# Fixed engine orders at two layer borders, and expert weights loaded in pieces of 4 MB

## The chip, the core and the metric

The kernel runs on one core of a Trainium2 chip. The core has five engines that each work off a queue of instructions of their own: TensorE (PE, matmuls; its weight loads are listed as PEld), VectorE (DVE), ScalarE (ACT), GpSimd (POOL) and SyncE (SP), which here issues nearly all DMAs. The metric is the time of one execution on the device in microseconds; less is better. All data is float32, x is 256 tokens of 1024 features, and all weights are read from HBM once, 503 MB in all.

## The reference, cut to what matters

Two transformer blocks one after another. The first mixes by a gated unit and a forgetting attention and ends in a gated feed-forward layer; the second mixes by pooling, an mLSTM and attention, then attends to a memory of 256 tokens, and ends in 16 experts, each of which takes the 32 tokens that score highest for it.

```python
# block 1
h = rmsnorm(x, mix_pre_g);  proj = h @ w_in
...
x = x + rmsnorm(merged @ w_out, mix_post_g)
h = rmsnorm(x, ffn_pre_g)
x = x + rmsnorm((silu(h @ w_gate) * (h @ w_up)) @ w_down, ffn_post_g)
# block 2
hn = rmsnorm_2(x, norm_mix_g);  proj = hn @ w_in_2
...
x = x + concatenate([y_pool, y_mlstm, y_attn]) @ w_out_2
x = x + mem_cross_attn(rmsnorm_2(x, norm_mem_g), mem, ca_wq, ca_wkv, ca_wo)
x = x + ec_moe(rmsnorm_2(x, norm_ffn_g), router_w, w_gu, w_down)
return rmsnorm_2(x, final_norm_g)

def expert(xe, wgu, wd):              # xe 32 x 1024, wgu 1024 x 4096, wd 2048 x 1024
    ga, up = split(xe @ wgu, 2)
    return (silu(ga) * up) @ wd
```

Between a norm and its product stands a whole row of x: a token's 1024 features must be summed in square before any of them can be scaled.

## The kernel before

**Dense layers.** x stays in SBUF as two tiles of 128 tokens (t = 0, 1). Weights come in units of 1 MB through three raw slots (`unit`, `unit_c`, lines 47 to 57), all on SP's queue. Each unit is split into a high and a low part by `split` (line 59): ACT copies the high part (line 67, in two halves), DVE subtracts it for the low part (line 68). The split units (`whl`) lie in four slots called hl. A product is made in three passes, high by high, low by high, high by low (`mm3`, line 86), with activations split in the same way (xh, xl). A norm (`norm_T`) squares on ACT (line 151), makes one over the root on DVE (`rstd`, lines 127 to 133: a guess on the bits and three steps of refinement, nine small operations and, with the sum at line 153, ten), scales x to hn (line 172), and has PE transpose hn (line 185); lines 118 and 119 copy the transposes into xh and xl.

**The two borders.** At border 1 (`block1_mix`, from line 414) the merged mixer output is multiplied by w_out for t = 0, then t = 1; each result goes through a norm (square, `pn` at line 201, rstd), is added to x (line 209), and is normalised again for the feed-forward layer. Beside it PE multiplies two units of block 2's memory keys (`mem_K`, tiles memH and memL), work that depends on nothing here. At border 2 (end of `block1_ffn`, line 577, and `block2_mix`, line 650) the same happens between the last three units of the down product (`tail`) and the first projections of block 2: keys and values (wk), then queries (wq), each for both tiles. After each of them ACT copies the result (lines 654 to 658).

**What sets the order.** A scheduler orders the instructions of each engine, from the order of the code and its own estimate of when each is ready; `queued` and the list `behind` (line 71) hold single instructions behind a named one. Engines wait for each other by semaphores.

**The experts.** `moe` (line 1068) has twelve slots of 2 MB (16 KB in each of 128 partitions): eight pools of its own and the four hl. `eload` (line 1088, issue at line 1091) puts the loads on SP's queue in one fixed order: for each expert eight of gate and up (128 rows of 16 KB each), then four of down. A slot is loaded again when PE is done with it. Per gate-and-up load PE does 16 matmuls (line 1163), on tokens that were gathered by matmuls with a one-hot matrix (line 1145). Then come silu and product (lines 1183, 1184), transposes (line 1187), the down products (line 1196) and the scatter back to the tokens (line 1210). The last expert's downs are loaded in pieces (line 1243): for three of the four the first 512 columns, then the rest, in rows of 2 KB; the fourth in four column cuts, so that little is left to do behind the last load. Then the final norm and two stores (line 1262).

## Time and profile before

| | |
|---|---|
| median of 3 runs | 1532.17 us (1532.10 to 1532.32) |
| the profiled execution | 1532.34 us, of which 1530.6 us lie between first and last instruction (the span) |
| mean granted TensorE clock | 0.890 |
| PE busy | 1194.9 us, 78% of the span |
| DVE, ACT busy | 430.8 us (28%), 349.6 us (23%) |
| moved by DMA | 503.0 MB, mean 329 GB/s |
| chain that ended last | 54% DMA, 2% PE, 2% SP's queue, 1% DVE |

The busy shares are means over stages that differ. Up to about 575 us PE is busy nearly throughout and the DMA moves 110 to 300 GB/s; from about 610 us the DMA moves 426 to 430 GB/s in each slice of the page and PE is busy for about 60% of the time. The chain is followed back from the last instruction, so its DMA share is the stage of the experts. Times in the trace count from the span's start. "Idle before" at a row is the time for which the engine had nothing to do ahead of it, and behind the arrow stands what ended that.

### The profile page before, as it was taken

The numbers are of one execution on the slowest core, as the hardware profiler recorded it, in microseconds if no ns is written. First come the engines' busy times: TensorE is split into PE (matmuls) and PEld (weight loads), VectorE is DVE, ScalarE is ACT, GpSimd is POOL, SyncE is SP. The second block draws the span as 40 slices with busy tenths as digits, with TensorE's granted clock in tenths as the row PEclk, the third lists the DMA queues.
The fourth block names the chain that finished last, engine by engine and source line by source line (L and its number), as shares of the span: only waits on it lengthen the run. The fifth ranks groups of instructions, "written<-read, shape, count | busy, mean of one in ns | idle before, by whom it ended". The sixth has DMA issues, their size and how long they took to land.

```text
span 1530.6 us, 17896 instructions
## 1 busy us (share of the span) xinstructions
PE 1194.9 (78%) x7704; PEld 677.5 (44%) x7704; DVE 430.8 (28%) x840; ACT 349.6 (23%) x604; POOL 7.0 (0%) x19
## 2 busy tenths in 40 slices
PE   7999998999999999886766666756656666567665
PEld 5988988999978786321121111111111112111112
DVE  6744666544577764300000000000000000000002
ACT  6554544443456733000000000000000000000002
POOL 1000000000000000000000000000000000000000
PEclk9999999999999999998877868789887789787798
DMA  9754446655533369999999999999999999999996
GB/s 302 223 165 147 156 150 220 193 187 187 178 114 109 111 235 429 399 428 426 427 428 427 428 427 428 426 429 426 428 426 428 426 428 428 426 428 426 428 424 245
DMA packets 109103, 503.00 MB, mean 329 GB/s; under 512 B 10059, under 2 KB 64095, under 8 KB 84960
## 3 DMA queue, kind: packets, MB, share of 16 engines
q1 hardware_dynamic: 109024, 501.86, 82.4%
q8 instruction: 60, 0.98, 0.3%
q14 instruction: 19, 0.16, 0.0%
HBM read 500.79 MB, written 1.05 MB: 328 GB/s over the span
## 4 chain that ended last, share of the span: by engine, by line
DMA 54%; PE 2%; SPq 2%; DVE 1%; issue 0%; ACT 0%; DVEq 0%
DMA eraw<-in_expert_w_gu_dram 36%; DMA eraw<-in_expert_w_down_dram 18%; SPq L1243 2%; PE sm L1163 1%; PE sm L1196 1%; PE sm L1145 0%; DVE tk L1117 0%; DVE m L1116 0%; PE acc L1210 0%; DVE OH L1129 0%; DVE x L1252 0%; ACT L1183 0%; PE sm L1187 0%; DVE es L1184 0%; DVE eraw L1260 0%
## 5 line engine op out<-in xcount | busy, mean ns | idle before, releaser
L1163 PE MATMUL sm<-eraw,xs 128*32 128x512 f32 x2048 | 323.9, 741 | 192.7 <-DMA eraw<-in_expert_w_gu_dram 192.7
L1163 PEld LDWEIGHTS sm<-eraw,xs 128*32 128x32 f32 x2048 | 62.4, 122 | 427.0 <-DMA eraw<-in_expert_w_gu_dram 291.9
L1196 PE MATMUL sm<-eraw,aT 128*32 128x512 f32 (+2 forms) x1088 | 173.4, 774 | 79.9 <-DMA eraw<-in_expert_w_down_dram 71.7
L68 DVE TENSOR_TENSOR whl<-raw,whl 128x1024 fp32r<-128x1024 f32 x166 | 198.8, 1220 | 113.2 <-ACT whl L67 112.5
L67 ACT ACTIVATE whl<-raw 128x1024 fp32r<-128x1024 f32 x166 | 168.3, 1052 | 84.7 <-issue 59.0
L1184 DVE SCALAR_TENSOR_TENSOR es<-sm,rsl,es 128x512 f32<-128x512 f32 x16 | 12.0, 751 | 465.6 <-PE sm L1163 462.6
L1196 PEld LDWEIGHTS sm<-eraw,aT 128*32 128x32 f32 x1088 | 34.7, 130 | 200.4 <-DMA eraw<-in_expert_w_down_dram 119.7
L1183 ACT ACTIVATE es<-sm,rsl 128x512 f32<-128x512 f32 x16 | 11.0, 687 | 426.8 <-PE sm L1163 426.8
L86 PE MATMUL acc<-xh,whl 128*128 128x256 f32 x704 | 95.6, 283 | 0.0
L86 PE MATMUL sm<-xh,whl 128*128 128x256 f32 x704 | 92.6, 284 | 1.1 <-ACT xh L118 1.1
L86 PEld LDWEIGHTS sm<-xh,whl 128*128 128x128 f32 x704 | 89.0, 192 | 1.9 <-ACT xh L118 1.3
L86 PEld LDWEIGHTS acc<-xh,whl 128*128 128x128 f32 x704 | 87.8, 189 | 1.1
L1208 DVE COPY ys<-sm 128x512 f32<-128x512 f32 (+2 forms) x18 | 11.4, 631 | 237.4 <-PE acc L1210 233.0
L86 PE MATMUL acc<-whl,xh 128*128 128x512 f32 x256 | 70.1, 404 | 1.1 <-DVE whl L68 0.8
L1210 PE MATMUL acc<-ys,ogT 128*128 128x512 f32 (+2 forms) x136 | 66.4, 612 | 5.1 <-DVE ys L1208 4.3
L1206 ACT ACTIVATE ys<-sm 128x512 f32<-128x512 f32 x16 | 9.6, 597 | 229.6 <-PE sm L1196 229.6
L86 PE MATMUL acc<-whl,aH 128*128 128x512 f32 x176 | 55.8, 390 | 0.0
L86 PEld LDWEIGHTS acc<-whl,xh 128*128 128x128 f32 x256 | 47.1, 189 | 14.2 <-DVE whl L68 2.2
L86 PE MATMUL acc<-xl,whl 128*128 128x256 f32 x352 | 49.7, 281 | 0.0
L86 PE MATMUL sm<-xl,whl 128*128 128x256 f32 x352 | 49.7, 284 | 0.0
L1210 PEld LDWEIGHTS acc<-ys,ogT 128*128 128x128 f32 x136 | 23.8, 198 | 53.2 <-issue 21.1
L86 PEld LDWEIGHTS sm<-xl,whl 128*128 128x128 f32 x352 | 45.6, 192 | 0.0
(364 smaller groups left out, 1098.4 us busy)
## 6 DMA issues: line engine op xcount, KB each, us to landing
eraw<-in_expert_w_gu_dram SPq DMA_DIRECT2D x128, 2048.0 KB, 39.2
eraw<-in_expert_w_down_dram SPq DMA_DIRECT2D x60, 2048.0 KB, 39.3
raw<-in_w_in_dram SPq DMA_DIRECT2D x34, 1024.0 KB, 5.4
raw<-in_w_gate_dram SPq DMA_DIRECT2D x11, 1024.0 KB, 5.4
raw<-in_w_up_dram SPq DMA_DIRECT2D x11, 1024.0 KB, 5.4
raw<-in_w_down_dram SPq DMA_DIRECT2D x11, 1024.0 KB, 5.0
raw<-in_w_out_dram SPq DMA_DIRECT2D x8, 1024.0 KB, 5.2
eraw<-in_expert_w_down_dram SPq DMA_DIRECT2D x7, 1024.0 KB, 27.7
```

What stands on the lines that cost most here:

```text
L67: nc.scalar.activation(H[:, k], raw[:, k], AF.Copy)
L68: self.at["L"] = nc.vector.tensor_tensor(L[:, k], raw[:, k], H[:, k].bitcast(F32), OP.subtract).ins
L86: nc.tensor.matmul(out, l[i], r[j], start=first and p == 0 and q == 0, stop=last and p == 2 and q == n - 1)
L1163: nc.tensor.matmul(dst[32 * j:32 * j + 32, :], xs[:, k, 32 * q:32 * q + 32], raw[:, o + 512 * j:o + 512 * j + 512], start=k == 0, stop=k = ...
L1183: nc.scalar.activation(s, G, AF.Silu, scale=rs)
L1184: nc.vector.scalar_tensor_tensor(s, U, rs, s, OP.mult, OP.mult)
L1196: nc.tensor.matmul(y[c0][32 * c:32 * c + 32, 0:n], aT[:, c, 32 * j:32 * j + 32], raw[:, o:o + n], start=j == 0, stop=j == 3, tile_position ...
L1206: nc.scalar.activation(ys, y[c0][:, 0:n], AF.Copy)
L1208: nc.vector.tensor_copy(ys, y[c0][:, 0:n])
L1210: nc.tensor.matmul(out[t], ogT[:, t * 128:(t + 1) * 128], ys, start=first, stop=last)
L1243: nc.sync.dma_start(raws[j].rearrange("p (i n) -> p i n", i=4)[:, :, c0:c0 + m], rows(j)[:, :, c0:c0 + m])
```

## The change

**Borders.** `strict()` ties each PE, DVE and ACT instruction that is written inside it to the one before it on its engine, so that the code's order is the engine's order. The code at both borders is written out anew in that order. Splits are placed half by half (`half_H`, `half_L`), a key unit's halves around the transposes of tile 1, and `rstd_q` takes the place of the bit guess: ACT makes the root, DVE a reciprocal and one step of refinement, five DVE operations and one ACT operation. At border 1 the raw weights of both key units and of the first gate unit are loaded ahead, and the first key unit is split before tile 1's out-projection. At border 2 the second key-and-value unit gets a split slot of its own (`whx`, pool `hx`), and the query product of tile 0 is cut in two around the transposes of tile 1.

**Experts.** The features are numbered anew (`feats`): piece k of x is every second column of a block of 256, so that two neighbouring pieces are the even and the odd rows of 256 rows of the weights. The pieces of experts 0 and 1 are still 2 MB in rows of 16 KB, now 32 KB apart in HBM. From expert 2 on one load brings two pieces, 4 MB in 128 rows of 32 KB; the eight pools are closed and four of 32 KB are opened in their place, and the four hl take the four downs. The router's weights and the gain are loaded in the same numbering. Of the last expert, downs 0 and 1 are loaded whole, in rows of 16 KB, and are used in all columns at once.

```diff
+def feats(k):
+    o = 256 * (k // 2) + k % 2
+    return slice(o, o + 255, 2)
...
+    def strict(self):
+        traced = self.nc.cur_bb.bb.instructions
...
+        for i in traced[start:]:
+            if i.engine in engines:
+                if at[i.engine] is not None:
+                    self.tc.add_manual_dep(i, at[i.engine].name, mybir.DependencyInfo(
+                        mybir.DependencyClass.NoSync, mybir.DependencyReason.DATA), reason="strict")
+                at[i.engine] = i
...
+    def rstd_q(self, ss):
...
+        nc.vector.tensor_scalar(v, ss[:, 0:1], ss[:, 1:2], 1.0 / D, OP.add, OP.mult)
+        nc.scalar.activation(d, v, AF.Sqrt, bias=self.eps)
+        nc.vector.tensor_scalar(h, v, -0.5, -0.5 * EPS, OP.mult, OP.add)
+        nc.vector.reciprocal(y, d)
+        nc.vector.tensor_scalar(t, y, y, h, OP.mult, OP.mult)
+        nc.vector.tensor_scalar(y, t, 1.5, y, OP.add, OP.mult)
...
+            raws = [self.unit_c(a["ca_wkv_2"][0], 256 * i) for i in range(2)] + [self.unit_c(a["w_gate"][0], 0)]
+            with self.strict():
...
+                self.post_norm_c(1, y, self.rstd_q(ss))
+                w.append(self.split_tile(raws[1]))
+                for i in range(2):
+                    self.split_half(w[1], raws[1], i)
+                ss = self.squares(self.xh(1))
+                self.mem_K(0, (w[0][:, 0], w[0][:, 1]))
+                ps = self.trans_ps(hs[0], "acc")
+                self.trans_H(xT[0], ps, 0)
+                hs[1] = scale(1, self.work.tile([128, D], F32, name="hn", tag="work"), self.rstd_q(ss))
+                kT = self.ps("sm")
+                self.mem_K_half(kT, 0, (w[1][:, 0], w[1][:, 1]))
...
+            HL = [self.split_tile(raws[0]), self.sb(self.hx, [128, 2, 4, 512], "whx", F32R)]
...
+            with self.strict():
+                out_k(0, self.gemm_t(xT, wk, 0))
+                acc = self.ps("acc")
+                self.gemm_part(acc, xT, wq, 0, 0)
+                ps = self.trans_ps(h, "sm")
+                self.trans_H(xT[0], ps, 1)
+                for q in range(2):
+                    self.trans_L(*xT, ps, 1, q)
+                self.gemm_part(acc, xT, wq, 0, 1)
...
+                if e == 2:
+                    est.close()
+                    e_ = [(self.open("ee%d" % i, 1, est, "right"), "e", 1) for i in range(4)]
+                    slots, n_unit[0] = [e_[1], e_[0], e_[2], e_[3]] + [hl] * 4, 0
                 for k in range(8):
-                    raw = eload(wgu[e, 128 * k:128 * k + 128, :])
+                    src = wgu[e, 256 * (k // 2):256 * (k // 2) + 256].rearrange("(p i) n -> p i n", i=2)
+                    if e < 2:
+                        raw = eload(src[:, k % 2])
+                    elif k % 2 == 0:
+                        both = eload(src.rearrange("p i n -> p (i n)"), 8192)
+                        raw = both[:, 0:4096]
+                    else:
+                        raw = both[:, 4096:8192]
...
+                    if j < 2:
+                        if i == 0:
+                            nc.sync.dma_start(raws[j], rows(j).rearrange("p i n -> p (i n)"))
+                            for o, w in cuts:
+                                down(j, raws[j], o, w)
+                        continue
```

DVE at border 1, from the addition of tile 1 to x on, before (pn is the out-projection times its gain, ss a sum of squares, hn the normalised x, xl the low part of transposes, whl a split unit):

```order
L209 SCALAR_TENSOR_TENSOR x<-pn,rstd,x 128x512 x2
L119 TENSOR_TENSOR xl<-sm,xh 128x4x128 x2
L153 TENSOR_TENSOR ss<-ss 128x1
L68 TENSOR_TENSOR whl<-raw,whl 128x1024
L127 TENSOR_SCALAR rstd<-ss 128x1
L68 TENSOR_TENSOR whl<-raw,whl 128x1024
L128 TENSOR_SCALAR rstd<-rstd 128x1
L129 TENSOR_SCALAR rstd<-rstd 128x1
L132 TENSOR_SCALAR rstd<-rstd 128x1
L68 TENSOR_TENSOR whl<-raw,whl 128x1024
L133 TENSOR_SCALAR rstd<-rstd 128x1
L68 TENSOR_TENSOR whl<-raw,whl 128x1024
```

DVE at the same place now:

```order
L294 SCALAR_TENSOR_TENSOR x<-pn,rstq,x 128x512 x2
L95 TENSOR_TENSOR whl<-raw,whl 128x1024 x2
L262 TENSOR_SCALAR rstq<-ss 128x1
L264 TENSOR_SCALAR rstq<-rstq 128x1
L265 RECIPROCAL rstq<-rstq 128x1
L266 TENSOR_SCALAR rstq<-rstq 128x1
L267 TENSOR_SCALAR rstq<-rstq 128x1
L216 SCALAR_TENSOR_TENSOR hn<-x,rstq,gain 128x512 x2
L237 TENSOR_TENSOR xl<-acc,xh 128x4x128 x2
L95 TENSOR_TENSOR whl<-raw,whl 128x1024
L237 TENSOR_TENSOR xl<-sm,xh 128x4x128 x2
L95 TENSOR_TENSOR whl<-raw,whl 128x1024
```

The six operations of rstd from ss to hn now stand in one row between a whole split and hn; before, splits lay between them, and hn itself came only six rows behind the last one shown.

PE at border 2, from the transposes of tile 0 to those of tile 1, before (xh and xl are the split transposes, acc a bank of results):

```order
L185 MATMUL sm<-ident,hn 128x128 x8
L86 MATMUL acc<-whl,xh 128x512 x5
L86 MATMUL acc<-whl,xl 128x512 x4
L86 MATMUL acc<-whl,xh 128x512 x8
L86 MATMUL acc<-whl,xl 128x512 x4
L86 MATMUL acc<-whl,xh 128x512 x7
L86 MATMUL acc<-whl,xl 128x512 x4
L86 MATMUL acc<-whl,xh 128x512 x8
L86 MATMUL acc<-whl,xl 128x512 x4
L86 MATMUL acc<-whl,xh 128x512 x4
L185 MATMUL sm<-ident,hn 128x128 x8
L86 MATMUL acc<-whl,xh 128x512 x4
```

PE at the same place now:

```order
L228 MATMUL sm<-ident,hn 128x128 x8
L127 MATMUL acc<-whl,xh 128x512 x4
L127 MATMUL acc<-whl,xl 128x512 x4
L127 MATMUL acc<-whl,xh 128x512 x4
L127 MATMUL acc<-whx,xh 128x512 x4
L127 MATMUL acc<-whx,xl 128x512 x4
L127 MATMUL acc<-whx,xh 128x512 x4
L127 MATMUL acc<-whl,xh 128x512 x4
L127 MATMUL acc<-whl,xl 128x512 x4
L127 MATMUL acc<-whl,xh 128x512 x4
L228 MATMUL sm<-ident,hn 128x128 x8
L127 MATMUL acc<-whl,xh 128x512 x4
```

The second key unit is read from whx, and the transposes of tile 1 now stand behind 36 and not behind 48 matmuls on tile 0.

SP at the end of the program, from the last expert's gate-and-up loads on, before:

```order
L1091 DMA eraw<-in_expert_w_gu_dram 128x4096 x8
L1226 DMA eraw<-in_final_norm_g_dram 1x1024
L1243 DMA eraw<-in_expert_w_down_dram 128x4x512 x7
L1243 DMA eraw<-in_expert_w_down_dram 128x4x256
L1243 DMA eraw<-in_expert_w_down_dram 128x4x128 x2
L1262 DMA out_dram<-eraw 128x1024 x2
```

SP at the same place now:

```order
L1230 DMA eraw<-in_expert_w_gu_dram 128x8192 x4
L1377 DMA eraw<-in_final_norm_g_dram 1x1024
L1395 DMA eraw<-in_expert_w_down_dram 128x4096 x2
L1401 DMA eraw<-in_expert_w_down_dram 128x4x512 x3
L1401 DMA eraw<-in_expert_w_down_dram 128x4x256
L1401 DMA eraw<-in_expert_w_down_dram 128x4x128 x2
L1420 DMA out_dram<-eraw 128x1024 x2
```

Four loads of 8192 columns are where eight of 4096 were, and two whole downs stand ahead of the pieces.

## Rows read from the trace of the kernel before

**Rows 1.** Page, chain that ended last, by line: share of the span.

```profile
DMA eraw<-in_expert_w_gu_dram 36%; DMA eraw<-in_expert_w_down_dram 18%; SPq L1243 2%; PE sm L1163 1%; PE sm L1196 1%; PE sm L1145 0%; DVE tk L1117 0%; DVE m L1116 0%; PE acc L1210 0%; DVE OH L1129 0%; DVE x L1252 0%; ACT L1183 0%; PE sm L1187 0%; DVE es L1184 0%; DVE eraw L1260 0%
```

**Rows 2.** Chain in order of time: start us, us, what.

```profile
656.83 30.94 DMA eraw<-in_expert_w_down_dram
```

**Rows 3.** Windows: us; PE, PEld, DVE, ACT, POOL busy; PEclk, DMA share, GB/s. Stream.

```profile
568.50:624.00 55.50, 52.11 (x261) 33.76 (x263) 31.14 (x99) 17.07 (x48) 0.38 (x2) 1.00 0.99 413
624.00:628.00 4.00, 4.00 (x38) 1.48 (x29) 0.29 (x1) 0.00 (x0) 0.00 (x0) 1.00 0.63 184
```

**Rows 4.** Waits of PE, border 2 to first expert: total, times, longest us.

```profile
PE sm L869 <- ACT AT L866: 1.1, 1, 1.1
```

**Rows 5.** Timeline of PE, border 1: start, us, instruction, count [idle, releaser].

```profile
224.81 2.06 PE L86 MATMUL sm<-memH,whl 128*128 128x256 f32 x16
...
230.50 1.03 PE L185 MATMUL sm<-ident,hn 128*128 128x128 f32 x8
231.29 2.15 PE L86 MATMUL sm<-memH,whl 128*128 128x256 f32 x16
...
241.13 1.29 PE L185 MATMUL sm<-ident,hn 128*128 128x128 f32 x8 [3.89 <-DVE hn L172]
243.50 4.00 PE L86 MATMUL sm<-xh,whl 128*128 128x256 f32 x17 [1.08 <-ACT xh L118]
...
249.00 2.12 PE L86 MATMUL sm<-xh,whl 128*128 128x256 f32 x16
```

**Rows 6.** Windows, same columns: PE's first half of the gate product.

```profile
242.30:249.10 6.80, 5.72 (x28) 5.60 (x27) 6.10 (x8) 3.87 (x5) 0.00 (x0) 0.50 0.64 214
```

**Rows 7.** Timeline of DVE and ACT, border 1.

```profile
222.16 0.15 DVE L153 TENSOR_TENSOR ss<-ss 128x1 f32<-128x1 f32 x1
...
224.31 0.60 ACT L151 ACTIVATE pj<-acc 128x512 f32<-128x512 f32 x1 [2.89 <-PE acc L86]
...
224.46 1.42 DVE L172 SCALAR_TENSOR_TENSOR hn<-x,rstd,gain 128x512 f32<-128x512 f32 x2
...
236.72 1.23 DVE L68 TENSOR_TENSOR whl<-raw,whl 128x1024 fp32r<-128x1024 f32 x1
...
240.23 1.42 DVE L172 SCALAR_TENSOR_TENSOR hn<-x,rstd,gain 128x512 f32<-128x512 f32 x2
...
244.90 1.28 ACT L544 ACT_TABLE_LOAD   x1
```

**Rows 8.** Waits of PE, border 2.

```profile
PE sm L185 <- DVE hn L172: 2.3, 2, 1.3
PE acc L86 <- DVE whl L68: 0.5, 1, 0.5
```

**Rows 9.** Timeline of PE, border 2.

```profile
432.63 1.29 PE L185 MATMUL sm<-ident,hn 128*128 128x128 f32 x8 [0.95 <-DVE hn L172]
...
460.59 1.10 PE L86 MATMUL sm<-xh,wgH 128*16 128x256 f32 x8
```

**Rows 10.** Windows, same columns: border 2.

```profile
431.50:460.60 29.10, 26.05 (x114) 19.42 (x114) 22.89 (x44) 14.42 (x28) 0.00 (x0) 1.00 0.44 130
```

**Rows 11.** DMA view, 700 to 1400 us; the last line: 1497 to 1506 us.

```profile
GB/s 429 427 428 426 428 426 428 428 428 426 428 427 425 432 424 430 426 427 429 423 432 424 429 428 425 429 425 427 429 426 430 425 428 427 426 428 427 427 428 427
DMA packets 20534, 299.06 MB, mean 427 GB/s; under 512 B 2280, under 2 KB 2280, under 8 KB 2280
...
q1 hardware_dynamic: 20510, 298.69, 100.4%
...
DMA packets 1756, 3.49 MB, mean 387 GB/s; under 512 B 54, under 2 KB 54, under 8 KB 1756
```

**Rows 12.** Timeline of PE, end of the last expert.

```profile
1491.12 3.25 PE L1163 MATMUL sm<-eraw,xs 128*32 128x512 f32 x16 [2.99 <-DMA eraw<-in_expert_w_gu_dram]
1496.05 1.92 PE L1163 MATMUL sm<-eraw,xs 128*32 128x512 f32 x16 [1.69 <-DMA eraw<-in_expert_w_gu_dram]
...
1501.49 4.48 PE L1196 MATMUL sm<-eraw,aT 128*32 128x512 f32 x24
```

More of the change, by code (lines that the diff above doesn't have):

```diff
@@ L76, in queued, with split_half, half_H, half_L @@
         return st
+    def split_half(self, HL, raw, s):
+        self.half_H(HL, raw, s)
+        self.half_L(HL, raw, s)
+    def half_H(self, HL, raw, s):
+        k = slice(s * raw.shape[1] // 2, (s + 1) * raw.shape[1] // 2)
+        self.nc.scalar.activation(HL[:, 0, k], raw[:, k], AF.Copy)
+    def half_L(self, HL, raw, s):
+        k = slice(s * raw.shape[1] // 2, (s + 1) * raw.shape[1] // 2)
+        self.at["S"] = self.nc.vector.tensor_tensor(HL[:, 1, k], raw[:, k], HL[:, 0, k].bitcast(F32), OP.subtract).ins
+    def split_tile(self, raw):
+        n, c = raw.shape[1:]
+        return self.big.tile([128, 2, n, c], F32R, name="whl", tag="hl", bufs=self.NH)
+    @contextmanager
+    def strict(self):
+        traced = self.nc.cur_bb.bb.instructions
+        last = traced[-1]
+        yield
+        at = {}
+        start = next(k for k in reversed(range(len(traced))) if traced[k] is last) + 1
+        engines = (mybir.EngineType.PE, mybir.EngineType.DVE, mybir.EngineType.Activation)
+        for e in engines:
+            at[e] = next((i for i in reversed(traced[:start]) if i.engine == e), None)
+        for i in traced[start:]:
[4 more added lines that the diff above has]
+                at[i.engine] = i
     def cols(self, w, c0):
@@ L194, in post_norm_a, with post_norm_b @@
         return self.rstd(ss, 1, 1.0 / D, "rsp")
-    def post_norm_b(self, halves, g):
-        y = self.work.tile([128, D], F32, name="pn", tag="work")
-        for i, h in enumerate(halves):
+    def post_norm_b(self, halves, g, y=None, o=0):
+        if y is None:
+            y = self.work.tile([128, D], F32, name="pn", tag="work")
+        for i, h in enumerate(halves, o):
             c = slice(i * 512, i * 512 + 512)
@@ L437, in block1_mix @@
-            trans(0, h[0])
-            self.behind = [(p["x", 1], p["q", 1])]
-            wg = self.split(self.unit_c(a["w_gate"][0], 0))
-            self.mem_K(2, w[1])
-            trans(1, h[1])
-            self.behind = [(p["E"], p["s", 1])]
+            acc = [[self.ps("acc") for _ in range(2)]]
+            self.out_part(units, (mH, mL), acc[0], 0, range(8))
+            ss = self.squares(acc[0])
+            y = self.post_norm_b(acc[0], gp)
+            self.post_norm_c(0, y, self.rstd_q(ss))
@@ L1223, in moe @@
                     nc.vector.tensor_tensor(x[:, t, c], x[:, t, c], acc[2 * t + n], OP.add)
-            end = slot()
+            end = e_[1][0].tile([128, 8192], F32, name="eraw", tag="e")
             grow, g, junk = end[0:1, 0:D], end[:, D:2 * D], end[:, 2 * D:3 * D]
```

188 lines of the change are left out of this document (122 added, 66 removed).

## The prediction

> **What bounds the kernel now.** I read the chain of waits first, by line and then in order of time. Over half of it is the DMA of the expert weights [rows 1], but only from 656.83 us on: what it goes back through there are loads in flight, the first for 30.94 us [rows 2]; the pieces ahead of it are work of PE, DVE and ACT. So there are two halves. In the first a late step on PE delays the rest; in the second only the rate of the stream of loads counts. The windows show how they are joined: the queue is nearly always full from 568.5 us on, sags in the four microseconds from 624, where the next loads wait for the first expert's slots, and is full again behind them [rows 3]. The thirteenth load and those behind it are issued as PE works off the first expert; when PE reaches it S us earlier, the whole stream is issued and lands S us earlier. No wait of PE between 460 and 625 us is one for a DMA (eleven kinds, the longest 1.1 us [rows 4]), so what PE gains at the two borders arrives there whole. The profiled execution took 1532.34 us; I subtract from that. The median is 1532.17.
>
> **Border 1 (out-projection to feed-forward).** In the timeline of PE, after the two key products, PE idles 3.89 us for the normalised tile 1 (hn), transposes, idles 1.08 us for the copy of the transposes, and runs the first half of the gate product in 249.00 - 243.50 = 5.50 us [rows 5]. The same 24 matmuls on the memory take (230.50 - 224.81) / 2 = 2.85 us [rows 5]. The window says why: behind that idling the granted clock is 0.50, the 1.2 GHz level [rows 6]. So the idle time costs 2.65 us more than itself.
> DVE is why hn is late. One rstd is ten small operations with the sum, 2.30 us on its own (224.46 - 222.16); that of tile 1 lies between four weight splits of 1.2 us each, and hn starts at 240.23 [rows 7]. The change gives the chain five small DVE operations and one ACT square root, and fixes the order: x, two halves of the second key split, rstd, hn.
> When is hn ready then? ACT's first square of the last out-projection bank starts at 224.31 and takes 0.60 [rows 7]; with the second and the reads of the sums, 225.75. The gain products on DVE and an rstd of 1.3 us (estimate: five operations of 0.2 and the hand-over to ACT and back) end at about 228.2, x (1.42) at 229.6. Then two split halves on DVE, beside the two squares on ACT: 231.9. The next rstd ends at 233.3, as ACT's copies stand ahead of its root; the two halves of hn at 234.0 and 234.7.
> When does PE want it? Its fixed row is key 0 (5.69), transposes of tile 0 (231.29 - 230.50 = 0.79), half of key 1 (2.85): 234.1. So the wait is 0 to 0.6 us, not 3.89. The copies of these transposes (1.08 before) hide behind the other half of key 1 (2.85). PE reaches the gate at 224.81 + 4 x 2.85 + 2 x 0.79 = 237.8, plus 0.3 of waiting, and with so little idling keeps the full clock: first half done at 240.95 instead of 249.00. **Gain 8.0 us.** Upper bound 8.35 (no wait). Lower bound 5.3: the clock falls anyhow, the 2.65 stay. One price is hidden: the square root may want its own function table on ACT, and a table load takes 1.28 us [rows 7]. It falls on tile 0's chain, while PE has all of the out-projection of tile 1 ahead of it; without that cover it would come off the gain.
>
> **Border 2 (feed-forward to block 2).** PE waits 2.3 us for hn (two times) and 0.5 for a split [rows 8]. It was done with the down product at 432.63 - 0.95 = 431.68, and the four products behind end at 460.59 [rows 9]: 28.9 us. They are 96 matmuls of 512 columns, each twice 2.85 / 24, so 0.237, or 22.8 us, and two transposes of 0.79: 24.4. So 4.5 us are lost in all, more than the listed waits. The granted clock is 1.00 throughout [rows 10]: no clock is to be won here. In the changed order hn of tile 0 is ready during the down product of tile 1; PE then still waits for a copy of its transposes, 0.6 us (as the ACT operation of that size [rows 7]). The transposes of tile 1 stand 36 matmuls later, at 433.1 + 8.5 = 441.6; by the chain of squares from 431.5 (with two copies between them, 2.4), rstd (1.4), x (1.42), squares (1.5), rstd (1.4), hn (1.42), hn is there at 441.0, and twelve matmuls cover the copies. The second key unit has a slot of its own, so the wait of 0.5 for a split goes. **Gain 4.5 - 0.6 = 3.9 us**; bounds 1.9 (hn of tile 1 comes two us late) and 4.5. What is late next: nothing down to the router, whose order is unchanged on all engines. The thirteen small constant loads that SP now issues behind the query weights are wanted only after 460 us. S = 11.9.
>
> **Loads of 4 MB.** From expert 2 on a gate-and-up load is 128 rows of 32 KB. With 16 KB rows the stream runs at 427 GB/s, in slices of 423 to 432; with the 2 KB rows of the last expert at 387 [rows 11]. No row of the trace is longer than 16 KB, so the price of a longer one has to be extended from these two. On one of 16 engines 16,384 bytes take 613.9 ns and 2,048 bytes 84.7: a straight line has 9.1 ns per row beside 36.9 ns per thousand bytes. 14 experts move 234.9 MB; 7,168 rows fewer are 448 per engine, x 9.1 ns = **4.1 us**. The bounds are what the slices show at either end: 550.1 us at 427 become 543.8 at 432 (+6.4) or 555.3 at 423 (-5.2). Nothing here says that a 32 KB row is carried as one packet; if it is carried as two, the term is near 0.
> The Trainium skill, "DMA: Bandwidth & Descriptors", section "Where 436 GB/s comes from", puts the ceiling at 435 GB/s; at that rate the 234.9 MB would take 540.0 us, 10.1 less than now. No slice here reached it.
> The queue doesn't run dry where slots change: each 4 MB load waits for two 2 MB uses of the old slots, and 10 MB or more are still queued then, some 24 us at 427 GB/s, against PE's 6.5 us for two such pieces at the half clock [rows 12].
>
> **The end.** The downs 0 and 1 of the last expert come in whole rows: 4.19 MB at 427 and not 387 GB/s, 1.0 us less. Against that PE gets the last two pieces of gate-and-up together at the time when it now gets the last one (1496.05), so it has 32 matmuls to do there and not 16: 1.92 us more at the full clock, 4.6 at the half one (6.5 and not 1.92); its downs start at 1503.4 to 1506 and not at 1501.49 [rows 12]. The two whole downs are some 4.3 us at the full clock, and the fourth's first piece lands only around 1511 (15.2 us of stream behind the last gate-and-up piece), so at the full clock the delay is absorbed; at the half clock it ends 1.7 us late. **Net +0.5**, bounds +1.0 and -1.7. The stride-2 slices that PE now reads as stationary data in the router and the first gather, some 16 instructions on the path: no such read stands in the trace; 16 transposes of contiguous columns take 1.6 us by [rows 5], and I take a fifth of that, **-0.3** (bounds 0 and, at the double, -1.6).
>
> **Sum.** 8.0 + 3.9 + 4.1 + 0.5 - 0.3 = 16.2; 1532.34 - 16.2 = 1516.1 us.
>
> **The rivals.**
> *Long rows bring nothing* (carried as two packets, or 427 is a ceiling that rows don't set): 1516.1 + 4.1 = 1520.2. For it: the queue's share is 100.4% already [rows 11]. Against it: 2 KB rows are slower. 0.17.
> *Half the border gain:* hn of tile 1 is late at one border, since ACT, in its fixed order, holds the square root behind the copies of transposes; half of S goes, 1522.1. For it: a strict order can't step around a late piece. Against it: the working above leaves 0 to 0.6 us of waiting. 0.10.
> *The end gives back:* the last 4 MB piece finds PE at the half clock: 1518.3. 0.06.
> *Slower: long rows are read more slowly.* The place is the stream from expert 2 on; it decides from the point where a 32 KB row takes over 2 x 613.9 ns + 12.1 us / 448 = 1254.8 ns, a rate below 417.8 GB/s; then all that the rest gains is gone. The nearest stretch with a lower rate is the first one of the experts, 413 GB/s [rows 3], though its start is a ramp. At 413 the 234.9 MB take 568.8 us, 18.7 more: 1532.34 - 12.1 + 18.7 = 1538.9. For it: half as many loads are queued, each twice as long on its engine. Against it: the slices vary by 1% only. 0.06, with two thirds of it slower than before by 0.2% and the rest between.
> *A fixed cost per load.* 299.06 MB in 700 us are some 142 loads, 4.93 us each, at the rate of full rows [rows 11]; what one load costs alone is hidden by those in flight beside it, so 56 loads fewer bring only what isn't hidden, at most 56 x (4.93 - 4.85 at 432 GB/s) = 4.5 us, and 1515.7. The Trainium skill, same page, section "Anatomy of one DMA — SWDGE (gpsimd) path", fits 2.0 us plus bytes at 436 GB/s for a load; 56 times 2.0 would be 112 us. By that fit 2 MB take 6.8 us, and the row's 4.93 speaks against it here. 0.01 for anything near it.
> *Better than the sum:* the rate of the 432 slices and no waits at the borders, 1512.5. 0.05.
>
> **How the numbers follow.** The forecast has 0.55, 1513 to 1518.5. The range takes in the first three rivals and the better case, 1511 to 1523, and leaves out the slow reads, 0.06, and the tails of the others. About 0.2% (3 us) is what can be told from no change here. Faster by over that: 0.93. Within: 0.03 (long rows eat 9 to 15 us). Slower: 0.04.
>
> **What would show it.** Border 1: PE's wait for hn below 1 us, none for the copies, granted clock 1.00 through the first gate product, gate begun 5 to 6 us earlier than 243.50. Border 2: the last product ends 12 us earlier than 460.59, of which 8 are border 1's. The thirteenth expert load is issued 12 us earlier. A rate of about 430 GB/s, so 9.75 us for each 4 MB, with 128 packets of data per load. The last downs wait for DMA, not for PE. The prediction is wrong if the clock still falls at border 1, if a wait for hn turns into one for the square root on ACT, or if the rate from expert 2 on lies below 425.

## The result, and the profile after

The changed kernel takes 1518.62 us (median of four, 1518.03 to 1519.82), the kernel before 1532.13 in the same comparison; the ratio is 0.9908, with a 95% interval of 0.9896 to 0.9920. The profiled execution took 1518.31 us, of which 1516.6 are the span, against 1532.34 and 1530.6. The forecast was 1516.1, in a range of 1511 to 1523: the direction and most terms hold, and 2.5 us are missing.

Border 1 first. The timeline of PE in the changed kernel, the rows that answer to [rows 5] (start us, us, instruction, count, and idle time before in brackets if there was any):

```profile
231.50 1.04 PE L228 MATMUL acc<-ident,hn 128*128 128x128 f32 x8
232.29 2.14 PE L127 MATMUL sm<-memH,whl 128*128 128x256 f32 x16
...
235.22 1.16 PE L228 MATMUL sm<-ident,hn 128*128 128x128 f32 x8
236.13 2.15 PE L127 MATMUL sm<-memH,whl 128*128 128x256 f32 x16
...
239.06 2.06 PE L127 MATMUL sm<-xh,whl 128*128 128x256 f32 x16
240.95 1.12 PE L127 MATMUL sm<-xl,whl 128*128 128x256 f32 x8
241.90 2.06 PE L127 MATMUL sm<-xh,whl 128*128 128x256 f32 x16
```

No row has a bracket: both waits are gone. The first half of the gate product takes 241.90 - 239.06 = 2.84 us where it took 5.50, and the window on it has the granted clock at 1.00 where [rows 6] had 0.50 (columns as there):

```profile
239.06:241.90 2.84, 2.84 (x26) 2.84 (x25) 2.33 (x3) 2.64 (x4) 0.00 (x0) 1.00 0.10 15
```

DVE and ACT in the same place, for [rows 7]:

```profile
232.34 0.21 DVE L262 TENSOR_SCALAR rstq<-ss 128x1 f32<-128x1 f32 x1
...
233.15 0.31 ACT L263 ACTIVATE rstq<-rstq,eps 128x1 f32<-128x1 f32 x1
...
233.49 0.16 DVE L265 RECIPROCAL rstq<-rstq 128x1 f32<-128x1 f32 x1 [0.75 <-ACT rstq L263]
...
234.24 1.42 DVE L216 SCALAR_TENSOR_TENSOR hn<-x,rstq,gain 128x512 f32<-128x512 f32 x2
```

hn starts at 234.24, not 240.23. DVE does wait 0.75 us for the root, which stands behind two copies on ACT, as the prediction had it; hn is still in time, since PE transposes it from 235.22 on without a wait.

Border 2, the timeline of PE, for [rows 9]:

```profile
425.71 1.16 PE L228 MATMUL sm<-ident,hn 128*128 128x128 f32 x8
427.00 1.20 PE L127 MATMUL acc<-whl,xh 128*128 128x512 f32 x4
...
435.48 1.16 PE L228 MATMUL sm<-ident,hn 128*128 128x128 f32 x8
436.39 1.17 PE L127 MATMUL acc<-whl,xh 128*128 128x512 f32 x4
...
450.47 1.08 PE L127 MATMUL sm<-xh,wgH 128*16 128x256 f32 x8
```

From the last down product to the end of the four products it is 450.47 - 425.71 = 24.8 us, before 28.9. But both borders together should have brought this end from 460.59 to 448.7; it stands at 450.47. Something else between them became slower.

The stream of the experts, for [rows 11], 700 to 1400 us:

```profile
GB/s 418 439 432 425 423 439 426 428 433 429 425 427 438 431 421 440 428 424 433 432 425 426 442 426 424 436 429 422 438 429 429 424 435 434 419 434 437 421 426 441
DMA packets 13792, 300.78 MB, mean 430 GB/s; under 512 B 1528, under 2 KB 1528, under 8 KB 1528
```

430 GB/s instead of 427, as far as the forecast went. A row of 32 KB is carried as one packet: in these 700 us the trace has 6,095 packets of 32,768 bytes, at a mean of 1219.3 ns, while the packets of 16,384 bytes in the kernel before take 616.4 ns each, 13.5 ns more for two of them. The packet count agrees: 300.78 MB are some 47.8 pairs of a 4 MB and a 2 MB load, and at 128 packets of data and 16 small ones each that is about 13,770. The slices of the first line swing by 24 GB/s mostly because the view counts a packet whole in the slice in which it starts: with each packet spread over the time that it took, the slices lie between 427.5 and 431.5 GB/s, and before between 426.1 and 428.4. So 423 and 432, which the prediction took as bounds of this term, were mostly counting as well.

### The profile page after: what moved, and what is told of

It reads as the page before. It is cut to its first block, busy times and chain, and to the rows that moved or that the text cites. A ratio compares the mean times of both kernels' runs of the same rounds, so it can differ in the third digit from the quotient of the medians.

```text
span 1516.6 us, 17752 instructions
## 1 busy us (share of the span) xinstructions
PE 1162.6 (77%) x7704; PEld 690.8 (46%) x7704; DVE 424.4 (28%) x801; ACT 355.5 (23%) x614; POOL 7.0 (0%) x19
## 4 chain that ended last, share of the span: by engine, by line
PE 70%; another core or an unknown queue 16%; DMA 5%; DVE 3%; SPq 2%; ACT 2%; issue 1%; DVEq 0%; ACTq 0%
PE acc L127 21%; PE sm L1314 18%; PE sm L127 10%; PE sm L1347 9%; PE acc L1361 4%; DMA eraw<-in_expert_w_down_dram 2%; DMA eraw<-in_expert_w_gu_dram 2%; SPq L1401 2%; PE sm L1284 1%; PE acc L1171 1%; PE sm L1338 1%; DVE es L1335 1%; DVE ys L1359 1%; ACT aT L1340 1%
## 5 line engine op out<-in xcount | busy, mean ns | idle before, releaser
L1314 PE MATMUL sm<-eraw,xs 128*32 128x512 f32 x2048 | 319.0, 779 | 222.9 <-DMA eraw<-in_expert_w_gu_dram 222.9
L1314 PEld LDWEIGHTS sm<-eraw,xs 128*32 128x32 f32 x2048 | 77.0, 138 | 447.4 <-issue 230.8
L74 DVE TENSOR_TENSOR whl<-raw,whl 128x1024 fp32r<-128x1024 f32 x152 | 181.7, 1221 | 105.9 <-ACT whl L73 104.8
L1347 PE MATMUL sm<-eraw,aT 128*32 128x512 f32 (+2 forms) x1088 | 145.1, 669 | 66.2 <-DMA eraw<-in_expert_w_down_dram 54.5
L73 ACT ACTIVATE whl<-raw 128x1024 fp32r<-128x1024 f32 x152 | 154.0, 1052 | 78.0 <-issue 47.2
L127 PE MATMUL acc<-whl,xh 128*128 128x512 f32 x240 | 65.9, 405 | 0.2
L1332 ACT ACTIVATE ogT<-sm 128x256 f32<-128x256 f32 x16 | 6.1, 383 | 220.6 <-PE sm L1330 220.6
L1361 PEld LDWEIGHTS acc<-ys,ogT 128*128 128x128 f32 x136 | 23.2, 193 | 59.8 <-DVE ys L1359 27.7
L127 PEld LDWEIGHTS acc<-whl,xh 128*128 128x128 f32 x240 | 44.6, 190 | 10.9 <-ACT xh L162 0.8
```

The costliest lines, as they stand in the source:

```text
L73: nc.scalar.activation(H[:, k], raw[:, k], AF.Copy)
L74: self.at["L"] = nc.vector.tensor_tensor(L[:, k], raw[:, k], H[:, k].bitcast(F32), OP.subtract).ins
L127: nc.tensor.matmul(out, l[i], r[j], start=first and p == 0 and q == 0, stop=last and p == 2 and q == n - 1)
L1314: nc.tensor.matmul(dst[32 * j:32 * j + 32, :], xs[:, k, 32 * q:32 * q + 32], raw[:, o + 512 * j:o + 512 * j + 512], start=k == 0, stop=k = ...
L1347: nc.tensor.matmul(y[c0][32 * c:32 * c + 32, 0:n], aT[:, c, 32 * j:32 * j + 32], raw[:, o:o + n], start=j == 0, stop=j == 3, tile_position ...
L1361: nc.tensor.matmul(out[t], ogT[:, t * 128:(t + 1) * 128], ys, start=first, stop=last)
```

## Where the time went, stage by stage

PE executes the same number of instructions in all kernels, up to the experts in the same order outside the borders, so the same matmul can be looked up in each trace. The table cuts each profiled execution at six fixed matmuls and two events. "Key" is the start of the first key product at border 1; "border 1" the next 144 matmuls, to within the second half of the first gate product; "dense" from there to three matmuls ahead of the end of the down product (the first two expectations below speak of a stretch that is 1.6 us longer); "border 2" from those three on over the four products, to ten matmuls ahead of their end; "to router" up to the routing of tile 1; "to 13th" up to the issue of the thirteenth expert load; "stream" up to the landing of the last gate-and-up piece; "end" what is left of the span. All in us. Each row is one execution, so differences of rows are not differences of medians.

| kernel | key | border 1 | dense | border 2 | to router | to 13th | stream | end | span |
|---|---|---|---|---|---|---|---|---|---|
| before | 224.8 | 25.1 | 180.9 | 27.4 | 156.5 | 10.2 | 871.1 | 34.6 | 1530.6 |
| changed | 225.8 | 17.0 | 182.2 | 23.1 | 157.7 | 10.1 | 866.2 | 34.4 | 1516.6 |
| x1_align64 | 224.4 | 16.9 | 178.9 | 23.1 | 156.1 | 10.2 | 866.4 | 35.7 | 1511.6 |
| x2_align128 | 227.0 | 17.2 | 182.4 | 23.2 | 156.1 | 11.8 | 866.4 | 35.7 | 1519.7 |
| x3_gu2mb | 225.9 | 17.1 | 182.4 | 23.1 | 156.5 | 11.7 | 870.7 | 34.5 | 1521.8 |
| x4_4mb_16k | 225.5 | 17.1 | 182.2 | 23.1 | 156.5 | 11.8 | 870.8 | 36.8 | 1523.7 |
| x5_border1 | 226.3 | 17.2 | 182.2 | 27.2 | 156.2 | 10.2 | 871.6 | 34.6 | 1525.6 |
| x6_border2 | 226.2 | 24.3 | 182.2 | 22.8 | 156.3 | 10.2 | 871.8 | 34.6 | 1528.4 |
| x7_end | 226.6 | 17.1 | 182.4 | 23.1 | 156.5 | 11.6 | 866.3 | 34.4 | 1517.9 |
| x8_moe | 224.9 | 25.1 | 180.9 | 27.4 | 156.5 | 10.2 | 866.3 | 35.8 | 1527.1 |
| x10_before_pad | 225.1 | 24.7 | 178.9 | 27.4 | 156.1 | 11.5 | 871.3 | 35.8 | 1530.6 |
| x11_pad_behind | 225.4 | 17.0 | 183.7 | 23.0 | 156.5 | 10.2 | 866.2 | 34.4 | 1516.5 |
| x12_after | 225.6 | 17.1 | 182.4 | 23.1 | 156.5 | 11.7 | 866.2 | 35.7 | 1518.2 |
| x13_align64 | 224.1 | 16.9 | 178.9 | 23.1 | 156.1 | 10.2 | 866.4 | 35.8 | 1511.6 |

Read the second row against the first: -8.1 at border 1, -4.3 at border 2, -4.9 in the stream, as forecast or better; but +1.0 ahead of border 1, +1.3 in the dense stretch, +1.2 up to the router, in code whose order the change leaves alone. These three are the miss.

The +1.0 ahead of border 1 has more than one part. PE's first matmul starts 0.24 us later, behind a longer wait for hn (total, times, longest), in the kernel before and then in the changed one:

```profile
PE sm L185 <- DVE hn L172: 10.7, 1, 10.7
```

```profile
PE sm L244 <- DVE hn L216: 10.9, 1, 10.9
```

Then 0.63 us grow along the 1,447 pairs of matmuls whose starts lie within 0.4 us of each other in both, and 0.13 in the few pairs further apart. The column differs between executions, too: it is 225.4 to 226.6 in the six that have whl where the change has it. The granted clock first rises to 1.00 at 15.5 us in the changed kernel and at 16.9 in x7, and x7 is about 0.7 us further behind from there on.

Two columns take two values with nothing between: "to 13th" 10.1 to 10.2 or 11.5 to 11.8, "end" 34.4 to 34.6 or 35.7 and more. The section on the clock below shows what goes with the higher value.

## The experiments

### The address of the operands: x1, x2, x11, x10

The dense stretch is work of PE without a wait, at a granted clock of 1.00, yet it takes longer in the changed kernel. The theory: the change puts new small tiles among the constants, ahead of the pool of split weights. In the built program eps takes 32 bytes per partition and the squares' scratch 1024, so whl and all behind it move by 1056 bytes: from 64 to 96 modulo 256. The rival: the pitch differs by run or through the new order.

```diff
-        self.eps = self.sb(per, [128, 1], "eps")
+        self.eps = self.sb(per, [128, 32], "eps")[:, 0:1]
```

> Only the size of the new constant eps is changed, from 1 to 32 floats per partition, so that all tiles behind it lie where their addresses modulo 128 bytes were before the change (64, not 96). Theory A (the matmuls of the feed-forward are 0.7% slower in the changed kernel because their operands moved to an address of 96 modulo 128): the stretch from the second half of the first gate product to the end of the down product is 182.5 us again, not 183.8, and the total is 1.3 to 1.7 us less than the changed kernel's, about 1517.1. Rival (the pitch differs for another reason, by run or by the new order): 183.8 us, total 1518.6.

Measured: 1513.37 us, ratio to before 0.9870 (0.9855 to 0.9884). Better than expected: the stretch is 178.9 us, 2.0 less than even the kernel before, although whl is at 64 modulo 128 in both. Modulo 256 it is at 192 here. x2 has the same line with 16 floats:

> eps with 16 floats per partition: the weight slots start at 0 modulo 128 bytes. Theory A: the feed-forward stretch is 182.5 us or less, the total 1517.1 or less. Rival: 183.8 us and 1518.6.

Measured: 1520.26 us, 0.9911 (0.9896 to 0.9926); the dense stretch 182.4, and the key product starts 1.2 us later still. So "128-byte aligned" is not better; the expected "182.5 or less" of the longer stretch is missed, and the theory in its first form, that a larger alignment is the faster one, fell. That the address matters stands: x1 and x2 differ by 64 bytes in it and in nothing else. That neither waits nor the clock make the difference, a window of 50 us shows (columns as above). The kernel before:

```profile
300.00:350.00 50.00, 50.00 (x358) 47.11 (x356) 24.53 (x24) 20.91 (x24) 0.00 (x0) 1.00 0.59 189
```

The changed kernel, in about the same place:

```profile
293.00:343.00 50.00, 50.00 (x354) 47.06 (x354) 24.12 (x25) 20.32 (x24) 0.00 (x0) 1.00 0.58 185
```

x1_align64:

```profile
293.00:343.00 50.00, 50.00 (x363) 47.12 (x362) 25.11 (x24) 21.10 (x24) 0.00 (x0) 1.00 0.59 189
```

PE is busy for all of it in each, at a granted clock of 1.00. The counts (358, 354, 363) go the way of the stretch, but are no measure by themselves: the windows don't begin at the same matmul, and they mix shapes. The measure is the time between the same two matmuls, in the table. Which operand is it? x11 moves only what lies behind whl:

```diff
+        self.padp = self.sb(self.open("padp", 1), [128, 24], "pad")
+        self.nc.vector.memset(self.padp[:, 0:1], EPS)
         self.rawp = self.open("rawp", 1, rawst)
```

> The changed kernel with 96 unused bytes behind the pool of the split weights: whl stays where the change has it (96 modulo 256), while raw weights, norms, gains and the feed-forward's activations behind it lie as in the run with eps of 32 floats (192 modulo 256). If the address of whl is what sets the pitch: feed-forward stretch 182.2 us, total 1518.6. If it is that of the other tiles: 178.9 us and about 1514.

Measured: 1518.91 us, 0.9913 (0.9898 to 0.9928), and a dense stretch of 183.7 us, longer than either. Taken apart by the mean distance of starts of consecutive matmuls, the gate and up products (stationary operand whl, moving operand xh or xl, whose place never changes) have 119.8 ns here, 119.7 to 120.0 in the changed kernel and the others with whl at 96, 116.7 in x1, 118.7 before, 120.1 in x2, 119.9 in x5 (whl at 224): they follow whl's address alone, and 96, 128 and 224 can't be told apart. The down products (whl against the activations aH, aL, which moved) have 233.9 ns here and 227.5 to 228.2 in the others, where both operands lie alike modulo 256. So in the down products the place of the activations counts too, and moving one operand alone can cost more. It is not the work beside PE: between matmuls with DVE and ACT both idle the distance is 119.8 ns in the changed kernel and 116.7 in x1, with both busy 119.6 and 116.7, and for the down products of x11 234.8 and 233.5. What in the hardware makes it so is open; no rule by which a place could be chosen without measuring comes out of five places of whl.

Last, the kernel before with an unused tile of 1152 bytes, which puts whl at 192:

```diff
+        self.pad = self.sb(per, [128, 288], "pad")
+        nc.vector.memset(self.pad[:, 0:1], EPS)
```

> The kernel before, with an unused tile of 1152 bytes per partition among the constants, and no other edit: all tiles behind it move, the split weights whl from 64 to 192 modulo 256 bytes. Theory A (the pitch of the matmuls depends on where their operands lie): the feed-forward stretch falls from 180.9 to 178.9 us, and the key product of border 1 begins 0.4 us earlier; total 2 to 2.8 us less than before. Rival (the run with eps of 32 floats was faster for another reason): 180.9 us, total as before.

Measured: the dense stretch is 178.9 us and the gate and up products are at 116.7 ns, exactly as in x1, with none of the change's code. That settles the address for this stretch. The rest of the expectation was missed. The key product begins 0.3 us later and not 0.4 earlier: its closely spaced matmuls bring 0.7, but 0.8 are lost in pairs further apart, nearly all at PE's start, where the granted clock rises at 16.7 us and not at 13.6. The total is only 0.12% less, 1.8 us instead of 2 to 2.8 (1531.2 us, 0.9988, 0.9979 to 0.9997). The profiled execution, at 1532.4 us slower than the median, has both higher values (11.5 and 35.8 in the table), 2.5 us that take the gain back; the ten executions spread from 1527.8 to 1532.6.

### Rows or loads: x3, x4

x3 keeps loads of 2 MB to the end, in the new numbering of features:

```diff
-                if e == 2:
+                if e == NE:
...
-                    if e < 2:
+                    if e < NE:
```

> The changed kernel with gate-and-up loads of 2 MB to the end (rows of 16 KB, 32 KB apart in HBM, the twelve slots of before); borders and the last expert's whole downs as in the change. Long rows (each row has a fixed price beside its bytes): the stream falls back from 430 to 427 GB/s and the total is 4 to 5 us longer, about 1523. Rival (the rate has another cause): no change, 1518.6.

Measured: 1524.0 us, 0.9941 (0.9924 to 0.9958), 0.0033 or 5.1 us above the changed kernel's ratio; the stream takes 870.7 us instead of 866.2. The DMA view, 700 to 1400 us:

```profile
DMA packets 20537, 299.10 MB, mean 427 GB/s; under 512 B 2280, under 2 KB 2280, under 8 KB 2280
```

That is the packet count and the rate of the kernel before, though the rows now lie 32 KB apart in HBM; the distance costs nothing that can be seen (870.7 us against 871.1). x4 has loads of 4 MB, each with 256 rows of 16 KB, and the old numbering:

```diff
-    return slice(o, o + 255, 2)
+    return slice(128 * k, 128 * k + 128)
...
-                    src = wgu[e, 256 * (k // 2):256 * (k // 2) + 256].rearrange("(p i) n -> p i n", i=2)
+                    src = wgu[e, 256 * (k // 2):256 * (k // 2) + 256].rearrange("(i p) n -> p i n", i=2)
...
-                        both = eload(src.rearrange("p i n -> p (i n)"), 8192)
+                        both = eload(src, 8192)
```

> The changed kernel with loads of 4 MB as in the change, but without the new numbering of features: each load brings 256 rows of 16 KB (two blocks of 2 MB), and PE reads contiguous slices. If the gain is one per row: 427 GB/s and 4 to 5 us longer, less 0.3 to 0.5 for the contiguous slices, about 1522.8. If it is one per load: 430 GB/s and 1518.2.

Measured: 1524.37 us, 0.9939 (0.9924 to 0.9954), stream 870.8. The DMA view:

```profile
DMA packets 19777, 299.10 MB, mean 427 GB/s; under 512 B 1520, under 2 KB 1520, under 8 KB 1520
```

As many loads as in the change (the 1520 small packets are 16 for each), as many rows as before, and the rate of before. The gain is one per row, not per load: half as many gate-and-up loads moved nothing (870.8 us in x4, 870.7 in x3). The fixed cost of 2.0 us a load by the Trainium skill ("DMA: Bandwidth & Descriptors", "Anatomy of one DMA — SWDGE (gpsimd) path"), a fit for loads that GpSimd issues, doesn't show in this stream, which SP issues with the loads queued behind each other.

### One border at a time, and the experts alone: x5, x6, x8

x5 is the kernel before with `block1_mix` of the change and the helpers that it calls (`strict`, `rstd_q`, `split_half` and their like, and the tile eps). Its core:

```diff
-            for t in range(2):
-                acc = [self.ps("acc") for _ in range(2)]
-                self.out_part(units, (mH, mL), acc, t, range(8))
-                r = self.post_norm_a(t, acc)
...
+            with self.strict():
+                ss = self.squares(self.xh(0))
+                hs[0] = scale(0, self.work.tile([128, D], F32, name="hn", tag="work"), self.rstd_q(ss))
+                w = [self.split_tile(raws[0])]
...
```

> The kernel before with border 1 alone rewritten as in the change. The stretch of PE from the first key product to 144 matmuls on, 25.1 us before and 17.0 in the changed kernel: 17.0 here. Border 2 27.4 us and the stream's 427 GB/s as before. Total: 8 us less than before if nothing else moves; if matmuls depend on the address of the split weights (here 224 modulo 256 bytes, before 64), the feed-forward stretch of 180.9 us moves by up to 2 us either way and the total is 6 to 10 us less.

x6 is the kernel before with the same helpers, but with `block1_ffn` and `block2_mix` of the change and `block1_mix` of before:

```diff
-            wk = [self.split(raws[0])]
...
+            HL = [self.split_tile(raws[0]), self.sb(self.hx, [128, 2, 4, 512], "whx", F32R)]
...
+                self.gemm_part(acc, xT, wq, 0, 0)
+                ps = self.trans_ps(h, "sm")
...
+                self.gemm_part(acc, xT, wq, 0, 1)
```

> The kernel before with border 2 alone rewritten as in the change. The stretch from the transposes of tile 0 over the four products, 27.4 us before and 23.1 in the changed kernel: 23.1 here; border 1 25.1 as before. Total: 4.3 us less than before if nothing else moves; with the split weights at 224 modulo 256 bytes, as in the run of border 1 alone, the feed-forward stretch is that of that run, and the total 2 to 6 us less.

Measured: border 1 alone has 17.2 us in its column, border 2 alone 22.8 in its own, and the other column stays (27.2, and 24.3 against 25.1). So each border works by itself. But the totals are 1527.93 us (0.9969, 0.9959 to 0.9979) and 1530.6 (0.9988, 0.9979 to 0.9997), 4.8 and 1.8 us less than before by the ratios, where the columns say 7.9 and 4.6; both are less than expected (6 to 10 and 2 to 6). In the profiles the rest is the key product, 1.4 to 1.5 us later, the dense stretch, 1.3 longer, and the stream, 0.5 to 0.7 longer. The dense stretch goes with the address, as the same small tiles stand ahead of whl, at 224 modulo 256 here. Of the delay ahead of the key product only 0.4 to 0.6 us are in closely spaced matmuls; 0.5 to 0.8 are lost at PE's start, where the granted clock rises at 17.2 and 16.6 us, and 0.2 to 0.3 ahead of its first matmul. Which part of a border's rewriting brings how much (the order, the shorter rstd, the loads or the slot of their own) was not tried. x8 takes `moe`, `route` and the router's loads alone, with no new tile:

> The kernel before with the experts' part of the change alone (numbering of features, 4 MB loads, whole downs), borders and addresses of the dense part as before. Stream at 430 GB/s instead of 427: 4 to 5 us less than before, plus 0 to 0.5 at the end, less 0.3 for strided slices. Feed-forward stretch 180.9 us, no slower matmuls. If the addresses alone slow the dense part, nothing else is lost here; if the strided reads cost 1 us or more in the router and the first gather, only 3 to 4.

Measured: 1527.6 us, 0.9968 (0.9957 to 0.9979), 4.9 less. Dense stretch 180.9 and key at 224.9 as before, stream 866.3, and the way to the router and on to the thirteenth load 156.5 and 10.2, as before: the strided slices cost nothing that can be seen, 0.3 had been taken.

### The end: x7

```diff
-                    if j < 2:
+                    if j < 0:
```

> The changed kernel with all four downs of the last expert in pieces, as before (rows of 2 KB). The prediction took 0.5 us of gain from whole rows there (1.0 less of DMA, part of it given back by the later start of the downs): 0.5 longer, 1519.1 against 1518.6. Rival (PE's late start ate it all): within 0.2 us. A loss of over 1 us would say that the late start costs nothing.

Measured: 1519.06 us, 0.9913 (0.9898 to 0.9928). The total can't tell the two expectations apart: it is 0.4 us longer, within the intervals, and the profile has 0.8 us more ahead of border 1. By the column, one execution each, the end takes 34.4 us with pieces and 34.4 with whole rows, so nothing is won there and the rival of the expectation holds. The 1.0 us of DMA was saved: in the packets the last data land 20.2 us behind the last gate-and-up piece with whole rows and 21.2 with pieces. Why it doesn't shorten the end, the timelines of PE show. The changed kernel:

```profile
1482.14 5.84 PE L1314 MATMUL sm<-eraw,xs 128*32 128x512 f32 x32 [4.38 <-DMA eraw<-in_expert_w_gu_dram]
...
1491.50 4.52 PE L1347 MATMUL sm<-eraw,aT 128*32 128x512 f32 x72
1497.30 1.06 PE L1347 MATMUL sm<-eraw,aT 128*32 128x512 f32 x8 [1.28 <-DMA eraw<-in_expert_w_down_dram]
1499.14 1.98 PE L1361 MATMUL acc<-ys,ogT 128*128 128x512 f32 x4 [0.78 <-ACT ys L1357]
1501.06 1.73 PE L1347 MATMUL sm<-eraw,aT 128*32 128x256 f32 x40
```

x7_end, with pieces of all downs:

```profile
1483.51 5.87 PE L1314 MATMUL sm<-eraw,xs 128*32 128x512 f32 x32 [4.44 <-DMA eraw<-in_expert_w_gu_dram]
...
1492.90 3.64 PE L1347 MATMUL sm<-eraw,aT 128*32 128x512 f32 x32
...
1499.24 1.94 PE L1347 MATMUL sm<-eraw,aT 128*32 128x256 f32 x48
1502.27 1.08 PE L1347 MATMUL sm<-eraw,aT 128*32 128x256 f32 x24 [1.09 <-DMA eraw<-in_expert_w_down_dram]
1503.68 1.20 PE L1347 MATMUL sm<-eraw,aT 128*32 128x256 f32 x16 [0.34 <-DMA eraw<-in_expert_w_down_dram]
```

With whole rows PE's last wait for a DMA ends at 1497.30, and from there PE, ACT and DVE set the end. With pieces PE has the first columns of all downs behind it earlier, and waits for the later pieces, up to 1503.68. What whole rows save in the queue, PE has left to do when they land.

### The clock between router and first expert: x12, x13

The changed kernel and x1, once more, on one chip:

> The changed kernel once more, for a comparison on one chip with the next run. Feed-forward stretch 182.2 us. In four of five profiles with its addresses or those of whl at 0 modulo 128 the granted clock fell for 1.2 to 1.6 us of loss between the router and the first expert's third piece; if that belongs to the moment at which PE gets there, it is seen here again (router to the thirteenth load 15.2 to 15.9 us, not 14.2). Total 0.991 of before.

> The changed kernel with eps of 32 floats once more (whl at 192 modulo 256), on the same chip as the run before. Feed-forward stretch 178.9 us, router to the thirteenth load 14.2 us, total 0.987 of before, 4 to 6 us less than the changed kernel on this chip.

Measured: 1518.15 us (0.9905, 0.9889 to 0.9922) and 1513.67 us (0.9880, 0.9866 to 0.9895): 4.5 us between the medians, at the same order of all instructions. The profiled executions lie 6.6 us apart, as that of x12 is slower than its median: 3.5 us are the dense stretch, 1.5 the way up to the key product and 1.5 the column "to 13th" (the stretch of the two expectations begins 4 us ahead of that column). The filler matmuls that PE runs beside the router, in the kernel before and then in the changed one:

```profile
612.43 1.67 PE L1065 MATMUL acc<-identb 128*128 128x512 bf16 x7
```

```profile
602.30 2.92 PE L1203 MATMUL acc<-identb 128*128 128x512 bf16 x7
```

The same seven take 1.25 us more; the window on them, in the changed kernel, has a granted clock of 0.55:

```profile
602.30:605.00 2.70, 2.70 (x9) 0.93 (x9) 1.28 (x7) 0.46 (x2) 0.19 (x1) 0.55 1.03 413
```

In x12 it falls a little later, at the gather and the first expert's first piece (timeline of PE):

```profile
610.56 0.74 PE L1284 MATMUL sm<-OH,x 128*128 128x128 f32 x4 [0.38 <-DVE OH L1268]
612.14 1.22 PE L1284 MATMUL sm<-OH,x 128*128 128x128 f32 x4 [0.84 <-DVE xs L1287]
613.29 2.88 PE L1314 MATMUL sm<-eraw,xs 128*32 128x512 f32 x16
616.10 0.74 PE L1284 MATMUL sm<-OH,x 128*128 128x128 f32 x4
```

And the same rows of x13, where it doesn't:

```profile
605.14 0.74 PE L1284 MATMUL sm<-OH,x 128*128 128x128 f32 x4 [0.38 <-DVE OH L1268]
606.72 0.74 PE L1284 MATMUL sm<-OH,x 128*128 128x128 f32 x4 [0.84 <-DVE xs L1287]
607.39 1.92 PE L1314 MATMUL sm<-eraw,xs 128*32 128x512 f32 x16
609.24 0.74 PE L1284 MATMUL sm<-OH,x 128*128 128x128 f32 x4
```

The windows on them, x12 and then x13:

```profile
612.00:616.30 4.30, 4.16 (x21) 1.73 (x22) 0.71 (x3) 0.00 (x0) 0.00 (x0) 0.62 0.46 194
```

```profile
605.20:609.40 4.20, 3.35 (x25) 1.61 (x26) 2.09 (x10) 0.00 (x0) 0.00 (x0) 1.00 0.80 343
```

The instructions and the idle times ahead are the same, 0.38 and 0.84 us; the granted clock is 0.62 in the one, so that PE runs at 1.2 GHz for most of it, and 1.00 (2.4 GHz) in the other, and the thirteenth load goes out 1.4 us later. Of the 14 profiles seven lose 1.2 to 1.6 us here: the changed kernel (twice), x2, x3, x4, x7 and x10; in each of these the granted clock falls to 0.50 between the router and the thirteenth load, in none of the other seven. The expectation that it belongs to the moment at which PE arrives doesn't hold: x11 gets to the router at 605.7 us, x7 at 605.6, and only x7 loses. What decides between executions with the same work is open. The end has two values as well: its first scatter (the row at 1499.14 above, 1.98 us) takes 3.61 us in x12. The 36.8 us of x4 were not taken apart.

```profile
1499.42 3.61 PE L1361 MATMUL acc<-ys,ogT 128*128 128x512 f32 x4 [0.78 <-ACT ys L1357]
```

## Why the prediction was right, and where its sum was off

- **Border 1, 8.0 us: right.** 8.1 by the table, and by the steps given: no wait for hn, copies hidden, clock at 1.00, and the wait on ACT's root that was counted (0.75 us on DVE) off the path. x5 has it alone. The border began 1.0 us later than before, so the gate began 4.4 us earlier and not 5 to 6.
- **Border 2, 3.9 us: right, a little low.** 4.3 by the table, 4.1 by the rows above (28.9 against 24.8); the copies cost PE about 0.5 us instead of 0.6, and hn was there before PE wanted it.
- **Long rows, 4.1 us: right, a little low.** 4.9 in the stream; all profiles with them lie at 866.2 to 866.4 there, all without at 870.7 to 871.8. The straight line through 2 KB and 16 KB rows gave 9.1 ns per row; 4.9 us / 448 are 10.9, and 4.6 us against x4, which differs in the rows, are 10.3. x4 shuts out the rival by loads. The rival by which long rows bring nothing had 0.17 and the slower one 0.06; neither came.
- **The end, 0.5 us: wrong in size, 0.** The 1.0 us of DMA was right (20.2 against 21.2 us). The step that failed is the one that let it arrive at the end: behind 1497.30 PE waits for no DMA there. The rival "the end gives back" had its condition fulfilled, the half clock at the last 4 MB piece (5.84 us for 32 matmuls, near its 6.5), in the changed kernel and in x7 alike; the 1.7 us that it priced didn't come. **Strided slices, -0.3: 0** (x8).
- **What was not in the sum: -1.9 us of operand addresses** (0.6 ahead of border 1, 1.3 in the dense stretch), **-0.4 that are not** (0.24 ahead of PE's first matmul, 0.13 in pairs of matmuls further apart), **and -1.1 of clock** (1.2 up to the router, less 0.1 behind it). That the 0.6 are the address is not shown by itself; it fits with the 0.6 to 0.7 that this part gains in x1, x10 and x13. The step that failed is "what PE gains at the two borders arrives there whole", with "nothing" as what is late next. It looked for waits and for the order of instructions, and both are indeed unchanged but for the 0.24 us at the start; that matmuls in untouched code could become slower by 0.7% because new small tiles shift their operands was in no term and no rival. With these the sum is 8.1 + 4.3 + 4.9 - 2.3 - 1.1 + 0.2 (the end's column) = 14.1, against the 14.0 between the profiled executions; as the columns add up to the span, that is an account and not a test.
- **Luck:** borders and rows gained 17.3 us where 16.0 were forecast, and these 1.3 us hid a part of the miss.
- The thirteenth load went out 9.1 us earlier, not 12, for the same reason, and the last product of border 2 ended 10.1 us earlier, not 12; of the signs named for a wrong prediction none appeared.

A version better than both came out of it: the changed kernel with eps of 32 floats (x1, x13), 1513.4 to 1513.7 us.

## What to carry to other kernels

A change that adds or drops any tile moves the operands of all matmuls behind it; compare the distance between starts of the same matmuls in untouched code before and after, and try a few paddings before judging the change. In this stream, whose queue is nearly always full, the number of rows counted and not that of loads: choose a numbering of features that makes contiguous rows longer. Where PE idles in short pieces, as in the 0.38 and 0.84 us here, the clock can differ from one execution to the next; look at the column of the stage, not at the total, to tell a gain of 2 us.

## What the runs showed of the hardware that was not expected

The place of a matmul's operands in SBUF sets its pitch by up to 3%: 116.7 ns for 256 columns with the stationary weights at 192 modulo 256 bytes, 118.7 at 64, and 119.7 to 120.1 at 96, 128 and 224; for 512 columns 227.5 to 228.2 ns, and 233.9 when one of the two operands moved by 96 bytes. Rows of 32 KB stream at 430 GB/s and rows of 16 KB at 427, on 16 engines, each row as one packet. The Trainium skill ("DMA: Bandwidth & Descriptors", "Where 436 GB/s comes from") names 435 GB/s as a ceiling; the trace agrees, as no slice of 17.5 us lies above 431.5 once each packet is spread over the time that it took.
